# The filters' first transform step: one float32 product in place of three on hi + lo pairs

## The chip, the cores and the metric

The kernel runs on one core of a Trainium2 chip. The metric is the device time of one execution in microseconds. Five engines work side by side: TensorE (PE in the profile; its weight loads are PEld), VectorE (DVE), ScalarE (ACT), GpSimd (POOL) and SyncE (SP), which here issues most DMA transfers. Each engine takes its instructions in order.

## What is computed

One encoder block on 2048 tokens of width 1024: a combined input projection, attention on one half of the heads and a long convolution ("Hyena") on the other, an output projection, a mixture of experts and a gated embedding. The change lies in the long convolution's filters, which are made from weights alone and taken to the frequency domain:

```python
h = jnp.sin(freq2 * (h @ w_f2 + b_f2))
h = (h @ w_f3).reshape(L, HYENA_ORDER, 2, D_HYENA)       # L = 2048, order 2, 512 channels
h = h * decay[:, None, None, :]
h = h / (jnp.sum(jnp.abs(h), axis=0, keepdims=True) + EPS)
hf, hb = h[:, :, 0], h[:, :, 1]
circ = jnp.concatenate([hf[:1] + hb[:1], hf[1:], jnp.zeros_like(hf[:1]), hb[:0:-1]], axis=0)
return jnp.fft.rfft(circ, n=2 * L, axis=0)
```

## The kernel before, in words

A transform of 4096 points is done in two steps of matrix products: a first step over 128 points (the matrix `w1`, 128x128, the same for all columns) and a second step of small products with 32 matrices (`w2`). The filters' work is `stage_filter`: for each of eight groups (four blocks of 128 channels, two orders) `gen` makes eight tiles `g` of 128x512 float32 values (line 402) and sums their magnitudes (403), `norm` works out one over the sum and scales the eight tiles in place (lines 412 to 438; two tiles on VectorE, six on GpSimd, line 436, and last a correction of one row of tile 0, line 438), `fft1` is the first transform step and `fft2` the second. The parts of successive groups are interleaved: while `gen` makes group n, `fft1` works on group n - 1 and `fft2` on group n - 2.

TensorE multiplies in two modes here. A float32 operand is multiplied in full precision; such an instruction stands in the trace as two rows. A `float32r` operand is multiplied in one quick pass at less precision, and a product of nearly full precision is put together from three of them, on pairs hi + lo: hi*hi, lo*hi and hi*lo. `Kit.hi_lo` (lines 77 to 81) makes a pair: ScalarE casts the values to hi (line 80), and VectorE or GpSimd subtracts hi from the values (line 81). `fft1` does that for every tile `g` (pair `gh`, `gl`, one buffer each) and multiplies by the pair `w1h`, `w1l` of the matrix, which `hyena_consts` makes once; the three products gather in one PSUM bank (the tag `pm`, of which there is one for all the filter's work, `norm`'s small products among it), ScalarE copies the bank out (452) and a DMA writes it to DRAM (453).

At the same time runs the input projection, `stage_in`, in four quarters of 512 tokens: normalise and transpose the tokens (lines 168 to 178), then products on hi + lo pairs by three `float32r` matmuls at a time (lines 149 to 151), and for the convolution's channels a three-tap filter on VectorE (`acc`, lines 210 to 213) whose result TensorE transposes (220). The lo parts of its weights are made on GpSimd mostly (line 89). `interleave` writes the two sides' instructions in proportion to costs that they yield, and the framework's scheduler then sets the order on each engine. The Hyena stage (first product at line 505) needs the filters and the first channels; attention (741 onwards) comes from the projection's side.

Of the kernel before, what the change touches and what calls it, by code (L numbers as in the profile page):

```python
# [9 lines left out]
F32R = mybir.dt.float32r  # L10
# [8 lines left out]
P = 128  # L19
# [15 lines left out]
HB = 3  # L35
FI_LATE = 1.5
GB = 8
GHB = 1
RB, WB = 13, 8
LO_ENG = (0,)  # L40
LO_POOL = 0
# [278 lines left out]
def stage_filter(K, st, cns, consts, w_f1, b_f1, freq1, w_f2, b_f2, freq2, w_f3, bias, h_d, s_d):  # L320


    nc, tc = K.nc, K.tc
# [16 lines left out]
    with tc.tile_pool(name="fi_s", bufs=2, side=K.side) as ps_:  # L340
# [26 lines left out]
        for c in range(4):  # L367
            ps = psm.tile([P, 512], F32, tag="pm", name="ps")
# [6 lines left out]
            ps = psm.tile([P, 512], F32, tag="pm", name="ps")  # L375
# [8 lines left out]
    pw = pool("fi_w", 2)  # L384
# [56 lines left out]
    def fft1(o, b, st):  # L441
        for q in range(8):
            g = st["g"][q].rearrange("p a c -> p (a c)")
            gh = pw.tile([P, 512], F32R, tag="gh", name="gh", bufs=GHB)
            gl = pw.tile([P, 512], F32R, tag="gl", name="gl", bufs=GHB)
            K.hi_lo(gh, gl, g, nc.vector if q % 2 else nc.gpsimd)
            ps = psm.tile([P, 512], F32, tag="pm", name="ps")
            nc.tensor.matmul(ps, K.w1h, gh, start=True, stop=False)
            nc.tensor.matmul(ps, K.w1l, gh, start=False, stop=False)
            nc.tensor.matmul(ps, K.w1h, gl, start=False, stop=True)  # L450
            sg = pw.tile([P, 4, P], F32, tag="sg", name="sg")
            nc.scalar.copy(sg, ps.rearrange("p (a c) -> p a c", a=4))
            nc.sync.dma_start(s_d[o, b, :, q * 4:q * 4 + 4], sg)
            yield 0.9
# [19 lines left out]
    for n in range(10):  # L474
        b, o = n // 2, n % 2
        st = {}
        parts = [gen(o, b, st) if n < 8 else iter(()), one, two]
        for _ in range(8):
            for p in parts:
                yield next(p, 0.0)  # L480
        for p in parts:
            yield from p
        if n < 8:
            yield from norm(o, b, st)
        one, two = fft1(o, b, st) if n < 8 else iter(()), fft2((n - 1) % 2, (n - 1) // 2) if 0 < n < 9 else iter(())
# [102 lines left out]
def hyena_consts(K, pool, tmp, w1_c, w2_c, wb_c):  # L588
    nc = K.nc
    K.w1 = tmp.tile([P, P], F32, name="w1")  # L590
    K.w1h, K.w1l = [tmp.tile([P, P], F32R, name=f"w1{i}") for i in "hl"]
    K.w1d = pool.tile([P, P], F32, name="w1d")
    K.w2 = pool.tile([P, 32, 64], F32, name="w2")
    K.wb = pool.tile([P, 64], F32, name="wb")
    for t, c in ((K.w1, w1_c), (K.w1d[0:64], w1_c[0:64]), (K.w1d[64:128], w1_c[0:64]), (K.w2, w2_c), (K.wb, wb_c)):
        nc.sync.dma_start(t, c)
    K.hi_lo(K.w1h, K.w1l, K.w1)


class RopeTables:  # L600
# [23 lines left out]
class Attention:  # L624
# [15 lines left out]
    def pool(self, name, bufs, **k):  # L640
        return self.st.enter_context(self.K.tc.tile_pool(name=name, bufs=bufs, **k))
# [1153 lines left out]
def block_kernel(tc, A, out):  # L1795
# [11 lines left out]
    with ExitStack() as st:  # L1807
# [3 lines left out]
        s_hc, s_w = ExitStack(), ExitStack()  # L1811
        phc = s_hc.enter_context(tc.tile_pool(name="hc", bufs=1, side=K.side))
        consts = lambda tmp: hyena_consts(K, phc, tmp, A["c_w1"], A["c_w2"], A["c_wb"])
        W, ple = [], Ple(K, A["p"][0, 0], A["w_ple"][0], pp_d)
        K.filter_done = False
# [89 lines left out]
```

## Time and profile before

| | |
|---|---|
| median of 3 runs | 3180.53 us (3178.24 to 3187.92) |
| the profiled execution | 3189.39 us, its span 3187.4 us |
| TensorE busy over the span | 2893.6 us (91%) |
| VectorE, ScalarE, GpSimd busy | 2088.4, 1357.0, 1186.7 us |
| first and last product of the changed step | 142.3 and 636.0 us from the span's start |

The changed step lies between 140 and 640 us, a sixth of the span, and work of `stage_in` lies beside it all that time. A matmul's row in the trace shows how long it took from its start to its result; matmuls overlap, so what one costs TensorE is the time from its start to the start of the next.

### The profile page before, as it was taken

To read this page: it belongs to the slowest core of one execution; us is meant where nothing else is said; L and a number is where in the kernel's file an instruction comes from. 1 tells how busy PE (TensorE), PEld (TensorE's weight loads), DVE (VectorE), ACT (ScalarE), POOL (GpSimd) and SP (SyncE) were. 2 spreads that over 40 slices of the span, in tenths; PEclk is the share of its full clock that TensorE was granted. 3 is DMA by queue.
4 is the path that set the end of the run, shared out by engine and by line. 5 is a ranking of instruction groups with operands and counts; after the bars stand their busy time and mean duration, and the time that the engine had idled before them with its cause. 6 is when DMAs were issued, how large, how long until landed. Compare 5 with 4: busy or idle time off the path is not lost. (4 is left out here: it accounts for less than half of the span.)

```text
span 3187.4 us, 50724 instructions
## 1 busy us (share of the span) xinstructions
PE 2893.6 (91%) x19065; PEld 1942.2 (61%) x19065; DVE 2088.4 (66%) x2770; ACT 1357.0 (43%) x2040; POOL 1186.7 (37%) x1090
## 2 busy tenths in 40 slices
PE   7989898878899999759999999989999999998887
PEld 5767686655444453424444388866667777775766
DVE  5877767455687566527787644366667777775665
ACT  3343343432343334225444432245556666664332
POOL 1434544341365455228887543001111211221443
PEclk9999999888899999879999999989999999999998
DMA  6468797886656655651000254369789888997553
GB/s 195 145 205 254 229 276 216 229 267 199 200 176 180 190 163 167 179 170 32 18 18 10 65 167 142 140 216 320 249 275 351 293 300 285 308 333 245 178 179 112
DMA packets 471992, 627.48 MB, mean 197 GB/s; under 512 B 64597, under 2 KB 302984, under 8 KB 467262
## 3 DMA queue, kind: packets, MB, share of 16 engines
q1 hardware_dynamic: 451630, 568.73, 55.7%
q0 software_dynamic: 20112, 55.47, 5.4%
q8 instruction: 151, 2.47, 0.3%
q14 instruction: 99, 0.81, 0.1%
HBM read 462.45 MB, written 161.56 MB: 196 GB/s over the span
## 5 line engine op out<-in xcount | busy, mean ns | idle before, releaser
L1314 DVE TENSOR_TENSOR wl<-raw,wh 128x1024 fp32r<-128x1024 f32 x384 | 463.3, 1223 | 196.3 <-ACT wh L1309 187.5
L1309 ACT CAST wh<-raw 128x1024 fp32r<-128x1024 f32 x384 | 398.6, 1051 | 266.2 <-PE ps L1332 95.1
L829 POOL TENSOR_TENSOR sums<-e,sums 128x512 f32<-128x512 f32 x306 | 411.0, 1359 | 156.5 <-ACT e L810 152.1
L810 ACT ACTIVATE e<-ps 128x512 f32<-128x512 f32 x512 | 289.7, 597 | 345.7 <-PE ps L809 291.7
L743 DVE TENSOR_REDUCE mx<-pa 128x1 f32<-128x512 f32 x512 | 330.3, 682 | 111.7 <-PE pa L741 110.8
L819 PE MATMUL po<-e,v 128*64 128x512 f32 x1024 | 293.8, 627 | 3.5 <-ACT e L810 3.5
L1409 POOL DMA_DIRECT2D y_d<-ob x64 | 36.0, 565 | 590.0 <-DVE ob L1408 346.6
L1330 PE MATMUL ps<-wh,xt 128*128 128x512 f32 (+4 forms) x512 | 212.9, 416 | 6.8 <-ACT wh L1309 6.8
L1331 PE MATMUL ps<-wl,xt 128*128 128x512 f32 (+4 forms) x512 | 206.7, 404 | 5.9 <-DVE wl L1314 5.9
L1332 PE MATMUL ps<-wh,xt 128*128 128x512 f32 (+4 forms) x512 | 203.4, 397 | 0.0
L149 PE MATMUL ps<-xh,wh 128*128 128x512 f32 x384 | 155.4, 405 | 5.0 <-ACT U L205 5.0
L741 PE MATMUL pa<-kst,q 128*128 128x512 f32 x352 | 142.0, 454 | 18.3 <-DVE mx L743 12.9
L151 PE MATMUL ps<-xh,wl 128*128 128x512 f32 x384 | 154.4, 403 | 0.0
L150 PE MATMUL ps<-xl,wh 128*128 128x512 f32 x384 | 154.0, 401 | 0.0
L806 PE MATMUL ps<-q,kst 128*128 128x512 f32 x352 | 151.7, 431 | 0.0
L829 DVE TENSOR_TENSOR sums<-e,sums 128x512 f32<-128x512 f32 x110 | 123.9, 1133 | 35.4 <-ACT e L810 34.8
L809 PE MATMUL ps<-q,k 65*128 65x512 f32 x352 | 142.0, 403 | 4.8 <-DMA q<-mr 4.8
L89 POOL TENSOR_TENSOR wl<-raw,wh 128x2048 fp32r<-128x2048 f32 (+1 forms) x26 | 102.1, 3926 | 100.4 <-ACT wh L139 99.5
L741 PEld LDWEIGHTS pa<-kst,q 128*128 128x128 f32 x352 | 63.6, 193 | 121.9 <-DVE mx L743 66.8
L1336 PE MATMUL pr<-raw,xr 128*32 128x128 f32 (+1 forms) x2112 | 126.3, 303 | 1.6 <-DVE ob L1412 1.6
L1330 PEld LDWEIGHTS ps<-wh,xt 128*128 128x128 f32 (+4 forms) x512 | 95.6, 187 | 44.8 <-issue 14.3
L1279 POOL DMA_INDIRECT g<-h_d,idx x52 | 70.0, 1347 | 140.1 <-PE pt L1288 58.6
(379 smaller groups left out, 6761.0 us busy)
## 6 DMA issues: line engine op xcount, KB each, us to landing
raw<-in_w_gate_dram SPq DMA_DIRECT2D x128, 512.0 KB
raw<-in_w_up_dram SPq DMA_DIRECT2D x128, 512.0 KB
raw<-in_w_down_dram SPq DMA_DIRECT2D x128, 512.0 KB
h_f<-hs SPq DMA_DIRECT2D x256, 128.0 KB
ab<-h_f SPq DMA_DIRECT2D x32, 1024.0 KB
raw<-in_w_in_dram SPq DMA_DIRECT2D x30, 1024.0 KB
xt<-in_x_dram SPq DMA_DIRECT2D x32, 512.0 KB
dec<-in_c_decay_dram SPq DMA_DIRECT2D x64, 256.0 KB
```

Source lines behind the costliest of these rows:

```text
L149: nc.tensor.matmul(ps, lh, rh, start=(k == 0), stop=False)
L151: nc.tensor.matmul(ps, ll, rh, start=False, stop=(k == 7))
L741: nc.tensor.matmul(pa, qh[:, t * P:(t + 1) * P], self.kst[g][:, q * 512:(q + 1) * 512], start=True, stop=True)
L743: nc.vector.tensor_reduce(out=mx[:, t, q:q + 1], in_=pa, axis=AX.X, op=ALU.max)
L810: nc.scalar.activation(out=pe[:, i], in_=ps, func=AF.Exp, scale=0.125)
L819: mm = nc.tensor.matmul(po[H2[i]], v[:, kt, g * 64:(g + 1) * 64], pe[:, i], start=(kt == 0), stop=(kt == NT - 1), skip_group_check=True)
L829: acc[j][1].tensor_tensor(out=sums[j], in0=pe[:, i], in1=src, op=ALU.add)
L1309: nc.scalar.copy(hi, raw)
L1314: nc.vector.tensor_tensor(out=lo, in0=raw, in1=hi.bitcast(F32), op=ALU.subtract)
L1330: nc.tensor.matmul(ps[:m], xt[:, k, 0, :m], hv[:, j], start=(k == 0), stop=False)
L1331: nc.tensor.matmul(ps[:m], xt[:, k, 0, :m], lv[:, j], start=False, stop=False)
L1332: nc.tensor.matmul(ps[:m], xt[:, k, 1, :m], hv[:, j], start=False, stop=(k == 7))
```

## The change

The tile `g` goes to TensorE as it is, with `w1` as it is, in one float32 product. The pairs, their buffers and the two pairs of `w1` are gone, and with them 64 casts on ScalarE, 32 subtractions each on VectorE and GpSimd, and 192 matmuls, for which 64 float32 ones (128 rows of a trace) stand.

```diff
     def fft1(o, b, st):
         for q in range(8):
             g = st["g"][q].rearrange("p a c -> p (a c)")
-            gh = pw.tile([P, 512], F32R, tag="gh", name="gh", bufs=GHB)
-            gl = pw.tile([P, 512], F32R, tag="gl", name="gl", bufs=GHB)
-            K.hi_lo(gh, gl, g, nc.vector if q % 2 else nc.gpsimd)
             ps = psm.tile([P, 512], F32, tag="pm", name="ps")
-            nc.tensor.matmul(ps, K.w1h, gh, start=True, stop=False)
-            nc.tensor.matmul(ps, K.w1l, gh, start=False, stop=False)
-            nc.tensor.matmul(ps, K.w1h, gl, start=False, stop=True)
+            nc.tensor.matmul(ps, K.w1, g, start=True, stop=True)
             sg = pw.tile([P, 4, P], F32, tag="sg", name="sg")
...
 def hyena_consts(K, pool, tmp, w1_c, w2_c, wb_c):
     nc = K.nc
     K.w1 = tmp.tile([P, P], F32, name="w1")
-    K.w1h, K.w1l = [tmp.tile([P, P], F32R, name=f"w1{i}") for i in "hl"]
...
-    K.hi_lo(K.w1h, K.w1l, K.w1)
```

The scheduler sets a new order on every engine of the first stage. Lines of the changed kernel are one less than those of before up to line 443, and the product is its line 444.

TensorE at the second group, from the last product that `norm`'s sums need to the first products of `fft1`. Before:

```order
L420 MATMUL ps<-hb,rowb 128x128
...
L176 MATMUL pt<-ident,xn 128x128 x8
L422 MATMUL ps_1167<-acc,blk 1x128
L423 MATMUL ps_1167<-hb,rowb 1x128
...
L448 MATMUL ps<-gh,w1h 128x512
L449 MATMUL ps<-gh,w1l 128x512
L450 MATMUL ps<-gl,w1h 128x512
L176 MATMUL pt<-ident,xn 128x128 x8
L448 MATMUL ps<-gh,w1h 128x512
```

And now:

```order
L419 MATMUL ps<-hb,rowb 128x128
L175 MATMUL pt<-ident,xn 128x128 x4
...
L421 MATMUL ps_1115<-acc,blk 1x128
L422 MATMUL ps_1115<-hb,rowb 1x128
...
L444 MATMUL ps<-g,w_549 128x512 x3
L175 MATMUL pt<-ident,xn 128x128 x8
L294 MATMUL pd<-zt,w_551 64x128 x16
L444 MATMUL ps<-g,w_549 128x512
```

The first "..." of before holds 10 matmuls of the projection (128x256), the second 24; now the first holds 12 and the second 12. So fewer products stand between `norm`'s sums and the first product that needs a scaled tile, and three products of `fft1` follow one another with nothing between. Two groups of the eight have such a row of three. At all eight groups, counted from line 423 (now 422) to the first product of `fft1`, the projection's matmuls between are 34, 24, 27, 47, 24, 26, 47 and 24 before and 31, 12, 22, 20, 1, 49, 17 and 0 now; transposes and products of `gen` and `fft2` stand there too.

VectorE a little ahead of that place (`part` and `acc` are `gen`'s sums and the projection's three-tap filter). Before:

```order
L403 TENSOR_REDUCE part<-g 128x128
L226 COPY stg<-pt 128x4x128
L81 TENSOR_TENSOR gl<-g,gh 128x512
L402 TENSOR_TENSOR g<-pd,dec 128x512
L403 TENSOR_REDUCE part<-g 128x128
L210 TENSOR_SCALAR acc<-U,cw 128x512
```

And now:

```order
L402 TENSOR_REDUCE part<-g 128x128
L225 COPY stg<-pt 128x4x128
L401 TENSOR_TENSOR g<-pd,dec 128x512
L402 TENSOR_REDUCE part<-g 128x128
L209 TENSOR_SCALAR acc<-U,cw 128x512
```

The subtraction is gone from the middle; what stood behind it, the three-tap filter among it, is as it was.

## Rows read from the trace of the kernel before

**Rows 1.** Stretches: us, busy us of each engine (instructions), granted clock, DMA share, GB/s.

```profile
100.00:200.00 100.00, 85.17 (x624) 65.45 (x622) 86.77 (x97) 33.85 (x52) 42.23 (x49) 0.97 0.49 156
200.00:300.00 100.00, 92.47 (x863) 77.53 (x864) 70.15 (x76) 40.83 (x64) 45.20 (x41) 0.97 0.84 251
300.00:400.00 100.00, 82.83 (x686) 64.52 (x686) 78.53 (x85) 38.18 (x60) 47.84 (x53) 0.93 0.76 230
400.00:500.00 100.00, 96.45 (x898) 80.16 (x898) 66.78 (x72) 44.22 (x67) 42.08 (x39) 0.97 0.91 270
500.00:640.00 140.00, 115.16 (x980) 94.68 (x977) 86.40 (x90) 53.80 (x89) 58.91 (x56) 0.93 0.77 223
```

**Rows 2.** What TensorE waited for, 100 to 700 us: total us, times, longest.

```profile
PE pt L220 <- DVE acc L213: 26.8, 17, 5.7
PE ps L448 <- ACT gh L80: 9.0, 4, 3.5
PE ps L450 <- POOL gl L81: 7.7, 5, 2.5
PE ps L151 <- DVE xl L81: 6.8, 4, 2.0
PE ps L450 <- DVE gl L81: 4.8, 3, 3.1
```

**Rows 3.** Instruction groups of the changed step: busy us, mean ns, idle before.

```profile
L448 PE MATMUL ps<-gh,w1h 128*128 128x512 f32 x64 | 30.6, 478 | 10.6 <-ACT gh L80 9.0 <-ACT sg L452 1.5
L80 ACT CAST gh<-g 128x512 fp32r<-128x512 f32 x64 | 39.7, 621 | 99.4 <-DVE g L438 37.9 <-PE ps L449 37.0 <-POOL gl L81 14.6
L81 POOL TENSOR_TENSOR gl<-g,gh 128x512 fp32r<-128x512 f32 x32 | 48.9, 1529 | 62.0 <-ACT gh L80 55.3 <-PE ps L151 6.4 <-PE ps L450 0.3
L81 DVE TENSOR_TENSOR gl<-g,gh 128x512 fp32r<-128x512 f32 x32 | 30.1, 941 | 33.8 <-ACT gh L80 22.9 <-PE ps L450 10.8
L452 ACT COPY sg<-ps 128x512 f32<-128x512 f32 x64 | 37.6, 588 | 39.0 <-DMA s_f<-sg 17.9 <-PE ps L450 15.3 <-issue 5.0
```

**Rows 4.** TensorE in order of time at 188 us: start us, us, instruction [idle before].

```profile
188.14 0.28 PE L151 MATMUL ps<-wh,xl 128*128 128x256 f32 x1
188.26 0.40 PE L448 MATMUL ps<-gh,w1h 128*128 128x512 f32 x1
188.50 0.39 PE L449 MATMUL ps<-gh,w1l 128*128 128x512 f32 x1
188.73 0.40 PE L450 MATMUL ps<-gl,w1h 128*128 128x512 f32 x1
```

**Rows 5.** TensorE in order of time at 1238 us: one float32 product (L841).

```profile
1237.94 0.39 PE L809 MATMUL ps<-q,k 65*128 65x512 f32 x1
1238.26 1.04 PE L841 MATMUL pa<-osq,sel 128*32 128x512 f32 x2
1239.23 0.73 PE L741 MATMUL pa<-kst,qh 128*128 128x512 f32 x2
1239.89 1.13 PE L505 MATMUL ph<-z,w1d 64*128 64x512 f32 x4
```

**Rows 6.** TensorE in order of time at 203 us, head of the second group.

```profile
202.99 0.28 PE L151 MATMUL ps<-wh,xl 128*128 128x256 f32 x1
206.79 0.79 PE L448 MATMUL ps<-gh,w1h 128*128 128x512 f32 x1 [3.52 <-ACT gh L80]
```

**Rows 7.** VectorE at the same place, first and last of `norm`'s scaling.

```profile
196.37 0.95 DVE L426 RECIPROCAL inv<-inv 128x128 f32<-128x128 f32 x1
...
204.80 1.23 DVE L438 TENSOR_TENSOR g<-g,iv 1x128 f32<-1x128 f32 x1
```

**Rows 8.** VectorE, GpSimd and TensorE in order of time, 174 to 182 us.

```profile
174.56 4.36 DVE L210 TENSOR_SCALAR acc<-U,cw 128x512 f32<-128x512 f32 x1 [0.21 <-ACT U L205]
...
174.12 4.51 POOL L89 TENSOR_TENSOR wl<-raw,wh 128x2048 fp32r<-128x2048 f32 x1 [4.65 <-ACT wh L139]
...
181.57 1.12 PE L220 MATMUL pt<-ident,acc 128*128 128x128 f32 x4 [5.25 <-DVE acc L213]
```

**Rows 9.** All instructions of line 210: duration ns min/median/max, first and last start us.

```profile
L210 DVE TENSOR_SCALAR acc<-U,cw x48: 531/546/4445, 85.5 to 794.6; 128x513 f32<-128x513 f32 x36, 128x512 f32<-128x512 f32 x12
```

**Rows 10.** TensorE in order of time, first product of the Hyena stage.

```profile
695.90 1.09 PE L505 MATMUL ph<-z,w1d 64*128 64x512 f32 x2 [0.66 <-DMA raw<-in_w_in_dram]
```

More of the change, by code (lines that the diff above doesn't have):

```diff
@@ L37 @@
 GB = 8
-GHB = 1
 RB, WB = 13, 8
```

## The prediction

> **What bounds the kernel now.** I began with the stretches of 100 us, to see which engine is full where the changed step runs. From 100 to 640 us [rows 1] TensorE is busy 472 of 540 us; VectorE comes next with 389, ScalarE and GpSimd are less than half full. The five stretches are not alike: from 200 to 300 and 400 to 500 us TensorE is busy 92 and 96 of 100 us, and each us of matmul added there should be a us of time; in the other three it is idle for a sixth of the time and VectorE is nearly as busy. The whole first stage hangs on TensorE's queue, since what follows (line 505, attention) needs its products. So I count by what the change adds to that queue and what it takes out of its waits. Idle time of the other engines is worth nothing until TensorE waits for it.
>
> Next I read what TensorE waits for [rows 2]. The largest wait is for the three-tap filter on VectorE, 26.8 us. The changed step has three: 9.0 us for the cast `gh`, 7.7 and 4.8 for the subtraction `gl`. Last I read the groups of the step itself [rows 3]: ScalarE's casts are 39.7 us, the subtractions 48.9 on GpSimd and 30.1 on VectorE, 119 us of work that goes. But most of what these engines do here is idle time anyway; the casts' queue alone stood 99.4 us before them.
>
> **TensorE's work: +17 us.** Three `float32r` products of 512 columns, one behind the other, start at 188.26, 188.50 and 188.73 [rows 4]: 0.235 us each, 0.70 us for the three, 64 times 45 us. What takes their place is a float32 product of 512 columns. None with all 128 rows into all 128 columns of the array is in the trace; the nearest uses 128 rows into 32 columns, the next 64 rows into 128. The first starts at 1238.26 and the next instruction at 1239.23 [rows 5]: 0.97 us. It started 0.09 us later than the row ahead (1237.94) and its 0.235 us would have it, and the two `float32r` products behind it take 0.66 us to the next float32 one where 0.47 would do, so a change between the two kinds costs some 0.1 us. Alone among `float32r` products the new one thus costs 0.97 + 0.2 = 1.17 us. It does not always stand alone: `gen`, `fft2` and the transposes are float32 too, and counted over the new order up to line 505 the kinds change 217 times, where they changed 231 times. So 64 x 0.97 = 62 us, less 14 x 0.1, is 61 us: 16 us more than the 45. The granted clock of 0.93 to 0.97 [rows 1] stretches that to 17. The upper end is 64 x (1.17 - 0.70) = 30, if most stand alone; the lower 16.
>
> The Trainium skill ("FP8 and Floating Point Precision", TensorE Precision Notes) says that a true float32 product goes through the array in four passes, against this change. By that rule and the pass of rows 4 the product would cost 4 x 0.235 = 0.94 us and the term would be 64 x 0.24, some 15 us; the row has 0.97 and the term stays.
>
> **Waits for the subtraction: -12 us.** The third product waited 7.7 + 4.8 us for `gl` [rows 2], and nothing takes its place. The bounds are -12.5 and about -6: where VectorE was late because its whole queue was late, the wait moves to the next thing that TensorE needs from it.
>
> **Waits at the head of a group: +4 us.** The 9.0 us for `gh` are not the cast's. At the second group TensorE stood 3.52 us from 203 on [rows 6], and VectorE's scaling of the tiles, begun at 196.37, ended only at 206.03 with line 438 [rows 7]; the cast behind it (0.62 us [rows 3]) is all that the change takes out, 2.5 us over the four waits. Line 444 waits for line 438 as the cast did. And the new order puts less in front of it: at the second, fifth and eighth group, where it waited before, 12, 23 and 24 fewer matmuls of the projection, at 0.12 us (half of 0.235; 188.14 to 188.26 [rows 4]) 1.4 to 2.9 us each, some 7 us. That is +4 or 5 together. Bounds: -2.5 (VectorE's chain is no longer behind) and +10 (groups three, four and seven, which also lose cover, begin to wait). I take +4. While line 444 waits, the projection's products behind it on TensorE wait too, and the transposes of the next tokens with them.
>
> **Waits for the one bank: +3 us.** Two groups now have three products of `fft1` in a row. All of them write the one bank `pm`, so the second and third must wait until ScalarE has copied the one before out: 0.59 us [rows 3] and 0.16 us until the result is there (0.40 less 0.235 [rows 4]), with the hand-overs some 0.85 us, four times. Bounds 0 and +5.
>
> **VectorE's relief: -4 us.** VectorE loses 30.1 us of work and 33.8 us of standing before it [rows 3], 64 of 540 us, an eighth. If its lateness falls by as much, TensorE's waits for lines 213 and 81, 33.6 us [rows 2], fall by 4. Bounds 0 and -13. I don't take more, because the largest of these waits have another cause: line 210 takes 0.55 us as a rule and up to 4.45 [rows 9], and the 5.25 us wait at 176 us comes from one that took 4.36 us while GpSimd worked at a weight subtraction of 4.51 us [rows 8]. Those subtractions (line 89) stay.
>
> The Trainium skill ("SBUF — State Buffer", SBUF: two separate sides) says that GpSimd and some forms of VectorE instruction take a shared pair of ports in turn, each for a whole instruction. The trace agrees in rows 8. By that rule the 32 subtractions that leave GpSimd would free VectorE too, but only where one of them stood in its way.
>
> **The rest: -2 us or nothing.** Where TensorE waits for something that no product of its own has to come before, added work fits into the wait: it is idle for 68 of 540 us [rows 1], an eighth of 17. ScalarE's and GpSimd's relief is hidden behind TensorE at no gain; their releases in rows 2 are counted above. Transfers are the same in number and size. The matrix's own pair is two small instructions at the start, and its load is long done at 142 us. Behind 700 us TensorE's order is nearly the same row for row, so what is won or lost at the start is carried to the end.
>
> **The sum:** 17 - 12 + 4 + 3 - 4 - 2 = +6 us. The profiled execution took 3189.39 us, 9 above the median of its runs; the difference of one execution carries over to the median: 3180.5 + 6 = 3186.5 us, say 3186. A measurement of this kernel can tell about 0.3% from no change, some 9.5 us, so my forecast is no change, on the slower side.
>
> **Rivals.**
> - *TensorE is the bound nearly throughout, and the new product is dearer than its nearest row.* For it: 92 and 96% busy in two stretches [rows 1], and the upper price of 30 us. With -12, +6 at the heads, +3 at the bank and nothing from VectorE it is +27 us, 3207; with the product at 1.0 us in place of 0.97, which is 2 us more, heads at +10 and nothing from VectorE, it is 19 - 12 + 10 + 3 - 2 = +18, 3198. It decides from about 3 us above my sum. Against it: most new products stand beside other float32 work.
> - *VectorE and the waits for the pairs were the bound.* It ends on the other side. For it: three of five stretches have VectorE at 62 to 87% [rows 1], and it stood 22.9 us waiting for `gh` and 10.8 for a free `gl` [rows 3], in a queue where the three-tap filter stands behind. If the waits for lines 213 and 81 fall by 13 us, the heads by 2.5 and the bank costs nothing: 16 - 12.5 - 2.5 - 13 - 2 = -14, 3166; with a little of the clock that the shorter waits give back (0.93 to 0.97 granted [rows 1], some 24 us lost in 540; a fifth of it) -19, 3162. It decides if VectorE's relief passes 15 us. Against it: the slow rows of line 210 stay, and the new order takes cover away.
> - *The change does what it says and no part meets the end:* the first stage's gain or loss is taken up where the Hyena stage waits for its transfers later. That is no change as well, 3180, and I count it with the forecast.
>
> **How the numbers follow.** No change 0.40 (the forecast and the third rival, 3171 to 3190); the first rival, slower, 0.38, centred on 3199; the second, faster, 0.22, centred on 3164. The likeliest case's own range is 3171 to 3190. With one in ten left out on each side the range is 3163 to 3208: the lower end is the second rival, the upper the first at its dearest.
>
> **What would show it.** In the changed profile line 444 should have 128 rows and 0.97 to 1.17 us from one product to the next instruction; a start-to-start of 1.3 us would make it slower. The waits on `gl` should be gone, a wait of line 444 for VectorE of 8 to 14 us stand in place of that for the cast, and one of some 3 us for the copy of line 452. The wait of line 220 for VectorE should still be above 15 us; if it falls below 10, the second rival holds. The first row of line 505, at 695.9 us before [rows 10], should come within 10 us of that; if it doesn't move but the time does, the cause lies behind and my account is wrong.

## The result: faster by half a per cent, and not where the change was made

| | before | after |
|---|---|---|
| median | 3183.21 us (10 runs) | 3170.03 us (10 runs, 3161 to 3179 without one) |
| ratio after / before | | 0.9947, 95% interval 0.9935 to 0.9959 |
| profiled execution, span | 3189.39, 3187.4 us | 3178.87, 3177.1 us |

One of the ten runs (3276 us, at a clock of 0.847 where the others had 0.95 to 0.96) is left out of the ratio. The forecast was no change, 3186 us; the kernel is 0.53% faster, outside the 0.3%, though inside the range.

**What the profile after shows of the changed step.** First the stretches of the kernel after (us, busy us of PE, PEld, DVE, ACT and POOL with instructions, granted clock, DMA share, GB/s), which answer to [rows 1]:

```profile
100.00:200.00 100.00, 86.24 (x578) 62.36 (x576) 83.03 (x96) 25.72 (x36) 43.17 (x48) 0.91 0.53 164
200.00:300.00 100.00, 91.69 (x878) 72.89 (x881) 51.22 (x60) 34.72 (x55) 19.97 (x16) 0.90 0.84 255
300.00:400.00 100.00, 85.19 (x600) 61.98 (x590) 74.25 (x75) 27.95 (x36) 44.14 (x56) 0.90 0.69 207
400.00:500.00 100.00, 92.39 (x878) 73.05 (x879) 53.44 (x65) 37.64 (x61) 23.65 (x20) 0.93 0.87 270
500.00:640.00 140.00, 119.48 (x908) 88.72 (x907) 84.25 (x91) 45.84 (x66) 45.44 (x62) 0.90 0.76 226
```

TensorE is busy 475 of 540 us, as before (472). VectorE has 346 in place of 389, ScalarE 172 in place of 211. The granted clock, 0.93 to 0.97 before, is 0.90 to 0.93 now. Next TensorE's waits from 100 to 700 us (total us, times, longest), for [rows 2]:

```profile
PE ps L444 <- DVE g L437: 19.6, 7, 6.1
PE ps L444 <- ACT sg L446: 13.5, 7, 3.8
PE pt L219 <- DVE acc L212: 9.4, 7, 2.9
PE ps L418 <- DVE acc L411: 8.3, 4, 3.4
```

The 12.5 us on `gl` are gone, and the wait for the three-tap filter fell from 26.8 to 9.4. In their place stand the head of a group (19.6 us, where the cast had 9.0), the one bank (13.5, where it had 1.5) and `norm`'s products, which wait for VectorE's sums (8.3, where they had 1.6). All told TensorE is idle for 65 of the 540 us; before it was 68. Third, TensorE in order of time:

```profile
165.38 1.02 PE L444 MATMUL ps<-g,w 128*128 128x512 f32 x2
165.84 0.79 PE L150 MATMUL ps<-xh,wl 128*128 128x512 f32 x1
166.47 0.39 PE L148 MATMUL ps<-xh,wh 128*128 128x512 f32 x1
...
170.82 1.02 PE L444 MATMUL ps<-g,w 128*128 128x512 f32 x2
171.77 1.10 PE L394 MATMUL pd<-w,h 64*64 64x128 f32 x32
...
195.77 2.06 PE L444 MATMUL ps<-g,w 128*128 128x512 f32 x2 [4.27 <-DVE g L437]
198.64 2.05 PE L444 MATMUL ps<-g,w 128*128 128x512 f32 x2 [0.81 <-ACT sg L446]
201.45 2.05 PE L444 MATMUL ps<-g,w 128*128 128x512 f32 x2 [0.77 <-ACT sg L446]
...
700.30 2.42 PE L499 MATMUL ph<-z,w1d 64*128 64x512 f32 x4 [1.60 <-DMA z<-uc_d]
```

Where a float32 instruction follows, the product takes 0.95 us to the start of the next (170.82 to 171.77), the price of [rows 5]. Among `float32r` products the next one starts 0.46 us after it, but then takes 0.79 us in place of 0.39; the one after that starts 1.09 us after the product, and less the 0.235 us of the one between, the product costs 0.85. So the time to the next start, by which this document prices a matmul, is too low there, and has to be read one instruction further on. At the second group the wait for VectorE comes as foretold, the clock falls behind it (the same product now lasts 2.05 us), and two waits of 0.8 us for the bank follow.

The Hyena stage starts at 700.30, 4.4 us *later* than in [rows 10]. That is not quite like for like: 44 products of the projection, 16 of line 699 and 8 transposes, which stood ahead of that mark before, stand behind it now. The first place behind the changed step up to which both kernels have done the same instructions on TensorE (the step's own products left out) is at some 760 us. A row soon behind it is easily found, a product of the projection that waits for ScalarE. Before and after:

```profile
777.55 0.79 PE L149 MATMUL ps<-xh,wh 128*128 128x512 f32 x1 [5.02 <-ACT U L205]
...
787.29 0.80 PE L148 MATMUL ps<-xh,wh 128*128 128x512 f32 x1 [4.06 <-ACT U L204]
```

Here the changed kernel is 9.7 us late, and 2.2 us in a second trace of it; the mean is what the sum said, +6. All that makes this execution 10 us shorter came after it.

**Where the time came from.** To see that, the table below gives how much later (+) or earlier (-) TensorE starts its work than in the trace of before: the start of an instruction in the one trace less that of the same instruction (the n-th of its line) in the other, as the median over all that lie within 12 us of the time at the head of the column. One trace each; two traces of one kernel differ by 9 us at 860 us and by up to 17 at the end. The column 778 is the start of the one product just shown. All kernels of the study are in it. The column "late order" says whose order TensorE has behind some 800 us (below). From there to the end, 667 of its 13,584 instructions stand in another place in the changed kernel (outside the longest common order), nearly all of them before 1300 us and from 2050 to 2250 us; in the kernel with pairs in (1,0) and in that with float32 in blocks 2 and 3 it is none.

| kernel | late order | ratio, 95% interval | 778 | 860 | 1300 | 1750 | 1830 | 2240 | end |
|---|---|---|---|---|---|---|---|---|---|
| after | after | 0.9947 (0.9935 to 0.9959) | +9.7 | +3.6 | +1.9 | +2.3 | -5.0 | -11.3 | -10.2 |
| after, second trace | after | 0.9951 (0.9932 to 0.9970) | +2.2 | -5.1 | -12.5 | -12.1 | -19.5 | -22.8 | -26.9 |
| float32 in seven groups, pairs in (2,0) | after | 0.9949 (0.9932 to 0.9966) | +6.1 | -4.3 | -8.6 | -10.3 | -16.2 | -22.3 | -19.1 |
| float32 in seven groups, pairs in (1,0) | before | 1.0013 (0.9997 to 1.0029) | +0.2 | 0.0 | +4.4 | +6.7 | +5.2 | +0.6 | +5.3 |
| half: float32 in blocks 0, 1 | after | 0.9903 (0.9887 to 0.9920) | -3.9 | -13.2 | -16.7 | -17.3 | -21.5 | -29.1 | -23.2 |
| the same, second trace | after | 0.9883 (0.9864 to 0.9901) | -5.3 | -11.7 | -3.1 | -2.0 | -6.1 | -14.6 | -11.5 |
| half: float32 in blocks 2, 3 | before | 0.9999 (0.9984 to 1.0014) | -2.5 | -6.1 | -2.4 | -1.0 | -2.6 | -5.4 | -2.3 |
| half: float32 in order 1 | after | 0.9944 (0.9927 to 0.9962) | +1.7 | -8.3 | -7.6 | -5.0 | -13.6 | -17.8 | -13.2 |
| pairs, two buffers each | after's behind 900, but for two rows | 0.9929 (0.9908 to 0.9950) | -9.0 | -11.7 | -10.8 | -10.2 | -8.5 | -12.5 | -12.6 |
| the same, casts moved | after's behind 900, but for two rows | 0.9948 (0.9928 to 0.9967) | -4.5 | -6.5 | -8.8 | -7.5 | -10.1 | -13.2 | -14.3 |
| half (blocks 0, 1), two buffers | after's behind 900 | 0.9882 (0.9861 to 0.9904) | -9.1 | -13.8 | -13.0 | -13.9 | -21.2 | -27.2 | -21.9 |
| before, casts moved | before | 0.9998 (0.9985 to 1.0011) | +0.4 | -1.8 | +4.0 | +4.7 | +3.4 | +4.1 | -0.3 |
| before, two rows swapped | before | 1.0004 (0.9992 to 1.0017) | +2.1 | -0.1 | +0.7 | +2.9 | +0.8 | -0.2 | -1.3 |
| before, transposes moved | before, but for the mixture of experts | 0.9997 (0.9983 to 1.0011) | +2.6 | 0.0 | +4.2 | +2.8 | +0.1 | +0.5 | +6.7 |
| before, all three moved | before, but for the mixture of experts | 0.9976 (0.9962 to 0.9991) | +0.4 | -1.9 | -1.8 | -3.4 | -6.0 | -10.5 | -9.1 |
| after, product issued twice | a fourth | 1.0052 (1.0030 to 1.0074) | +29.1 | +20.0 | +17.7 | +17.8 | +15.1 | +10.8 | +15.9 |
| after, pairs made but not used | a fifth | 0.9992 (0.9980 to 1.0004) | - | -1.6 | -12.8 | -2.1 | -2.8 | -3.4 | +1.7 |

In the first row 7.3 us are won between 1750 and 1830 us, the end of attention, and 6.3 up to 2240 us, the start of the mixture of experts. At the first of these places the trace of before has this (ScalarE, then TensorE, in order of time):

```profile
1797.68 1.08 ACT L810 ACTIVATE e<-ps 128x512 f32<-128x512 f32 x2 [0.53 <-issue]
1805.93 0.62 ACT L80 CAST th<-ya 128x512 fp32r<-128x512 f32 x1 [7.17 <-DMA ya<-ya_d]
1806.77 0.62 ACT L80 CAST th<-ya 128x512 fp32r<-128x512 f32 x1 [0.21 <-DMA ya<-ya_d]
1807.29 3.03 ACT L810 ACTIVATE e<-ps 128x512 f32<-128x512 f32 x6
...
1807.93 2.46 PE L819 MATMUL po<-e,v 128*64 128x512 f32 x4 [3.50 <-ACT e L810]
```

Two casts of the output projection stand in ScalarE's queue ahead of 14 of attention's exponentials and wait 7.17 us for a transfer; the exponentials behind them wait too, and TensorE for those. In the changed kernel the scheduler has put the same casts ahead of the last 6 only, and TensorE does not wait there in either of its traces. No line of the diff is near these; the scheduler, which sets the order of the whole program, had come to another one.

**The theories.** *Late order*: the gain is that of the order in which the scheduler set the instructions behind the first stage; the changed step is worth nothing by itself. *First stage*, the rival: the cheaper step and VectorE's relief are worth the 13 us, wherever a trace shows them. *Luck*, the second rival: transfers that landed earlier by chance.

### The profile page after: what moved, and what is told of

Its sections match the earlier page's. It is cut to its first block, busy times and chain, and to the rows that moved or that the text cites. A ratio compares the mean times of both kernels' runs of the same rounds, so it can differ in the third digit from the quotient of the medians.

```text
span 3177.1 us, 50424 instructions
## 1 busy us (share of the span) xinstructions
PE 2905.4 (91%) x19001; PEld 1937.3 (61%) x19001; DVE 2047.3 (64%) x2737; ACT 1322.0 (42%) x1975; POOL 1143.2 (36%) x1058
## 5 line engine op out<-in xcount | busy, mean ns | idle before, releaser
L148 PE MATMUL ps<-wh,xh 128*128 128x256 f32 x384 | 121.6, 317 | 4.7 <-ACT xh L79 2.4
```

The source lines that it names most:

```text
L148: nc.tensor.matmul(ps, lh, rh, start=(k == 0), stop=False)
```

## The experiments

**The changed kernel again, and one group more or less.** When the float32 product is used in some groups only, TensorE's order behind about 800 us (the last 3500 matmuls of attention and the start of the mixture of experts) comes out either as in before or as in after, row for row, and which one does not go by how many groups are changed. (That holds for TensorE. In the kernels with the late order of before, ScalarE and VectorE have some 150 rows each in another place behind 1300 us.)

> The changed kernel once more, for a second trace. Late order (the 10 us were won behind the changed step, because the scheduler set another order at the end of attention and at the start of the mixture of experts): the time is 3161 to 3173 again, the trace is again 2 to 5 us behind the kernel before at 700 us and at 1200 us, and gains 5 to 8 us at about 1800 us and 5 to 8 us between 2090 and 2210 us. First stage (the cheaper pairs and the relief of VectorE were worth it): the time is the same, but the gain is there by 1200 us. Luck (transfers that by chance landed earlier in one profiled execution): the steps at 1800 and 2200 us are not there again, or at other places.

> Seven of the eight groups have the float32 product, one (block 1, order 0) keeps its pairs. The orders behind the first stage (end of attention, start of the mixture of experts, everything after) are the ones of before, row for row. Late order: nothing is won late, and the first stage costs what it cost in the changed kernel, some +2 to +4 us: 3181 to 3189, a ratio of 0.999 to 1.002. First stage: seven eighths of the gain, 3168 to 3175, a ratio of 0.995 to 0.997. Luck: anything between.

> Seven groups with the float32 product and one with pairs, as in the earlier run of seven groups, but the one that keeps its pairs is block 2, order 0, in place of block 1, order 0. By that the order of the last 3500 matmuls of attention and the start of the mixture of experts is the one of the changed kernel and not of before. Late order: the gain is there, ratio 0.993 to 0.997, where the other gave 1.0013. First stage: the two are alike, both near 1.001.

```diff
-            nc.tensor.matmul(ps, K.w1, g, start=True, stop=True)
+            if (b, o) == (1, 0):
+                gh = pw.tile([P, 512], F32R, tag="gh", name="gh", bufs=GHB)
...
+                nc.tensor.matmul(ps, K.w1h, gl, start=False, stop=True)
+            else:
+                nc.tensor.matmul(ps, K.w1, g, start=True, stop=True)
```

That is the kernel with pairs in (1, 0), with the code of before between; the other has (2, 0) there.

Seven eighths of the change with the late order of before: 1.0013. Seven eighths with the late order of after: 0.9949, the whole gain. TensorE's waits in order of time, first of the kernel with pairs in (1,0):

```profile
1192.21 3.69 PE L308 MATMUL ph<-ab,wa 64*64 64x128 f32 x64 [6.13 <-issue]
...
1789.32 0.63 PE L844 MATMUL pa<-sums,sel 128*32 128x512 f32 x3 [2.31 <-POOL sums L832]
1815.65 1.56 PE L822 MATMUL po<-e,v 128*64 128x512 f32 x4 [2.44 <-ACT e L813]
...
2117.12 1.09 PE L1291 MATMUL pt<-ident,g 128*128 128x128 f32 x4 [7.17 <-DMA g<-h_d,idx]
```

and of the kernel with pairs in (2,0), the same stretches:

```profile
1806.04 1.65 PE L844 MATMUL pa<-sums,sel 128*32 128x512 f32 x6 [0.73 <-DVE sums L832]
...
2099.65 1.94 PE L1291 MATMUL pt<-ident,g 128*128 128x128 f32 x8 [4.37 <-DMA g<-h_d,idx]
```

The first has the waits of before at their places (there 4.5, 1.8, 3.5 and 4.9 us), the second those of after, where of the four only the gather's is left (3.6 and 5.3 us). The first stage theory falls here: at 778 us the kernel that wins is 5.9 us behind the other. Luck falls too: the stall near 1186 us stands in every trace with the late order of before and unchanged rows (4.5 to 6.5 us) and in none with that of after. One thing did not come as expected: the second trace of after was not 2 to 5 us behind, but 12.5 ahead at 1300 us. It had won 14.7 us since 778, where the first trace had won 7.8.

**Half and half, three ways.**

> Half and half, first of a pair: the float32 product for the four groups of blocks 2 and 3, pairs for those of blocks 0 and 1. On TensorE the order of the last 3500 matmuls of attention and of all behind it is the one of the kernel before. Late order (the gain comes from the orders behind 860 us, not from the first stage): no gain, ratio 0.999 to 1.002. First stage: half of the gain, ratio 0.997 to 0.998.

> Half and half, second of the pair: the float32 product for the four groups of blocks 0 and 1, pairs for those of blocks 2 and 3, so as many of each as in the first. The order of the last 3500 matmuls of attention and at the start of the mixture of experts is the one of the changed kernel. Late order: nearly the whole gain, ratio 0.994 to 0.997, and the steps in drift against before lie at 860 to 1240, near 1800 and between 2090 and 2210 us. First stage: half of the gain like the other half, ratio 0.997 to 0.998, and no difference between the two.

> Half and half in a third way: float32 for the four groups of order 1, pairs for those of order 0; the order late in the program is that of the changed kernel. Late order: a gain as of the half with blocks 0 and 1 (0.9903): 0.989 to 0.996. First stage: half the gain, 0.997 to 0.998. If half and half is better in the first stage than all float32, the drift at 860 us is again -8 to -13 us, where the changed kernel has +4 and -5.

The edit is the one above with `b < 2`, `b >= 2` or `o == 0` for the pairs. The pair of equal halves gave 0.9999 and 0.9903, the third 0.9944: again by the late order. From the row at 778 us to the end, the six traces with the late order of after gain 19 us on average (19.9, 29.1, 25.2, 19.3, 6.2 and 14.9); the three with that of before and rows unmoved lose 2 (0, 5.1 and 0.2). That is 21 us; by the ratios, whose means are 0.9930 and 1.0004, it is 24. By place, the difference is 7 us from 778 to 860 us, 4 from 860 to 1300, 5 from 1750 to 1830 and 3.5 from 1830 to 2240. I had not expected that half and half would be clearly better than the changed kernel.

**No changed product at all.**

> The kernel before with pairs in all groups and one number changed: two buffers for each of the pair tiles. The end of attention stands as in before (the casts of the out-projection ahead of 14 exponentials), the middle of attention and the mixture of experts in another order, the latter that of the changed kernel. Late order: most of the gain without the changed product, less the 3 to 7 us near 1800 us: ratio 0.995 to 0.998. First stage: a second buffer can only take away part of the 9.0 us wait for the cast: 0.998 to 1.000.

> The kernel before with pairs in all groups, the casts at the end of attention put where the changed kernel has them, and two buffers for each of the pair tiles (in place of one), by which the scheduler sets the order of the mixture of experts and of all behind it to that of the changed kernel. Late order: both late steps are won, 10 to 15 us, and the first stage is at most 5 us better or worse than before by the second buffer: 3166 to 3175, ratio 0.995 to 0.998. First stage: the late places are worth nothing, and the buffer at most removes part of the 9.0 us wait for the cast: 3178 to 3184, ratio 0.998 to 1.000. Luck: like the first stage.

```diff
-GHB = 1
+GHB = 2
...
-        K.hi_lo(th[:, 0:4], tl[:, 0:4], ya, nc.gpsimd)
+        c = nc.scalar.copy(th[:, 0:4], ya)
+        if t < 2:
+            K.behind(c, K.es[-7])
+        nc.gpsimd.tensor_tensor(out=tl[:, 0:4], in0=ya, in1=th[:, 0:4].bitcast(F32), op=ALU.subtract)
```

The first of them has the first line alone, the second both. With pairs in all groups and one buffer more they give 0.9929 and 0.9948, as much as the change, without it; the first is better than the 0.995 to 0.998 expected of both. At 778 us they are 9.0 and 4.5 us ahead, and behind it they win 3.6 and 9.8, so a good part of their gain is the second buffer's, in the first stage. TensorE's order behind 900 us is that of after but for two rows at the end of attention, and there, from 1750 to 1830 us, they won at most 2.6 us, where the kernels with all of that order won 4.1 to 8.6.

**The named waits one by one.** Which rows of the late order are it? Three edits of the kernel before, each meant to move only what I held to be the cause, and all three together. The swap does so. With the casts the scheduler also moved 163 of ScalarE's rows behind 1750 us, and with the transposes 149 of TensorE's rows in the mixture of experts.

> The kernel before, with pairs in all groups, and one edit at the end of attention: the first two casts of the out-projection's tokens on ScalarE are put behind the seventh exponential from the end, where the changed kernel has them (6 exponentials behind the first cast and not 14). Late order: TensorE's wait for an exponential at 1808 us (3.5 us, and a lower clock behind it) is gone and the time falls by 5 to 8 us, to 3174 to 3178, ratio 0.9975 to 0.9985; the step in drift at 1800 us is there with no change at 140 to 640 us. First stage: no change, 3183, ratio 1.000 within 0.001. Luck: no change either.

> The kernel before with one pair of neighbouring rows on VectorE in the other order: at about 1187 us the scaling of attention's fifth output (ob<-ob,gcol, which waits for a transfer) is put behind the Hyena product ab<-ab,ph that stood behind it. TensorE's order is the one of before. Late order, by the mechanism of a queue in which one instruction waits for a transfer and holds up the next: TensorE's wait of line 308 at 1186 us (4.5, 6.1, 6.5 and 5.1 us in the four traces with that order) falls below 2 us, and the drift against before steps by -3 to -6 us between 1180 and 1300 us; ratio 0.998 to 0.9995. If the wait only moves to the next transfer: no step, ratio 1.000.

> The kernel before with one edit at the start of the mixture of experts: the first transposes of the second gathered tokens on TensorE, which wait for the gather (4.9 to 9.0 us in the five traces with the order of before, 3.6 to 5.3 with that of the changed kernel), are put behind the first 16 of the products pr<-raw,xr, as in the changed kernel. By the named waits: the stall at 2105 us is 3 us shorter, and the drift against before steps by -3 to -5 us between 2050 and 2240 us; ratio 0.9985 to 0.9995. By the order as a whole: no step of more than 1.5 us, ratio 1.000.

> The kernel before with the three named corrections at once: the swap of two rows on VectorE at 1187 us, the two casts at the end of attention behind 8 more exponentials, and the transposes at the start of the mixture of experts behind 16 products. Pairs in all groups, the first stage as before. By the named waits: the sum of what the changed kernel won at these places, some -4, -5 and -4 us: ratio 0.995 to 0.997. By the order as a whole (each wait that is taken away here comes back a few rows on): at most -4 us, 0.9985 to 1.000.

```diff
+            if K.no == 5:
+                K.behind(gate, K.abs[47])
...
+                if K.nt == 9:
+                    K.behind(tr, K.prs[15])
```

The casts' edit is the one shown above. Here `gate` is attention's fifth `ob<-ob,gcol` and `K.abs[47]` the product `ab<-ab,ph` that stood behind it; `tr` is the first transpose of the second gathered tokens, `K.prs[15]` the 16th product `pr<-raw,xr`.

The swap at 1187 us shows best how such an edit can fail. VectorE and TensorE of before, in order of time:

```profile
1187.52 0.75 DVE L858 SCALAR_TENSOR_TENSOR ob<-ob,gcol 128x512 f32<-128x512 f32 x1 [6.65 <-DMA ob<-r_d]
1188.19 2.35 DVE L529 TENSOR_TENSOR ab<-ab,ph 128x1024 f32<-128x1024 f32 x2
...
1190.64 3.69 PE L308 MATMUL ph<-ab,wa 64*64 64x128 f32 x64 [4.49 <-issue]
```

and with the two rows swapped:

```profile
1182.94 2.35 DVE L531 TENSOR_TENSOR ab<-ab,ph 128x1024 f32<-128x1024 f32 x2 [0.37 <-PE ph L297]
1189.58 0.75 DVE L860 SCALAR_TENSOR_TENSOR ob<-ob,gcol 128x512 f32<-128x512 f32 x1 [4.29 <-DMA ob<-r_d]
1190.25 1.28 DVE L745 TENSOR_REDUCE mx<-pa 128x1 f32<-128x512 f32 x2
...
1187.78 1.98 PE L310 MATMUL ph<-ab,wa 64*64 64x128 f32 x64
1190.99 1.10 PE L743 MATMUL pa<-kst,q 128*128 128x512 f32 x2 [1.24 <-DVE mx L745]
```

Line 308 no longer waits, but the transfer is as late as it was, and what now stands behind the waiting instruction is the row maximum `mx`, for which TensorE waits next. From 1180 to 1300 us the step was 1.0 us, where 3 to 6 were expected; the time, 1.0004, shows none. The casts, of which 5 to 8 us had been expected, gave 0.9998: the wait at 1808 us is gone, and 20 us ahead of it TensorE stands 4.44 us where it stood 1.83 before:

```profile
1787.93 1.07 PE L842 MATMUL pa<-sums,sel 128*32 128x512 f32 x3 [4.44 <-POOL sums L830]
```

The transposes alone gave 0.9997. All three at once gave 0.9976 (7.7 us of 3193), between the two ranges expected and half of the changed kernel's gain, without a row of the first stage moved; of the wait for the gather (4.9 to 9.0 us with the late order of before, 3.6 to 5.6 with that of after) 1.59 are left (TensorE of that kernel):

```profile
1779.72 0.63 PE L846 MATMUL pa<-sums,sel 128*32 128x512 f32 x3 [2.88 <-POOL sums L834]
...
2107.78 1.07 PE L1299 MATMUL pt<-ident,g 128*128 128x128 f32 x8 [1.59 <-DMA g<-h_d,idx]
...
2113.40 0.51 PE L1344 MATMUL ps<-wh,xt 128*128 128x512 f32 x1 [3.11 <-ACT wh L1323]
```

So the named waits, with the rows that the scheduler moved along with them, are some 8 of the 21 us. About 4 more lie with a wait of TensorE at 1018 us (shown in the last section): between 999 and 1028 us each of the six traces with the late order of after wins 4.2 us. The rest lies with rows that I have not named.

**The first stage by itself.** Two kernels with the changed product: one issues each product twice (twice the step's work, the same output), one makes the pairs as before and uses them for nothing.

> The changed kernel with every product of the first step issued twice, the second over the first (the output is the same, the work of the step doubled): 64 more products at 0.97 us by the prediction, 62 us of TensorE. It asks how much of the first stage's work reaches the end. If it reaches it in full: the first product of the Hyena stage some 55 to 65 us later, and the time 3215 to 3235, ratio 1.008 to 1.015. If the stretches from 640 to 860 us take up a part, as they took up 8 us in the run with seven groups: 8 to 10 us less than at that first product. The order behind 860 us is partly that of the changed kernel, so up to 15 us may come off.

> The changed product, but the pairs are still made (casts and subtractions) and used by nothing: it leaves out the relief of the other engines and keeps the dearer product. The order behind 860 us is a third one, neither that of before nor of the changed kernel. If VectorE's relief is what paid for the dearer product in the first stage (TensorE's wait for the three-tap filter fell from 26.8 to 9.4 us in the changed kernel): that wait is again above 20 us, and the drift at 860 us is +8 to +20 us. If the relief is not the cause: the wait stays near 10 us and the drift at 860 us within 5 us of the changed kernel's (+4 and -5). The time itself tells little, since the late order is another.

The stretch from 100 to 640 us of after, of its second trace and of the kernel with the product twice:

```profile
100.00:640.00 540.00, 474.99 (x3826) 358.99 (x3825) 346.18 (x383) 171.88 (x254) 176.37 (x201) 0.91 0.74 224
...
100.00:640.00 540.00, 469.34 (x3895) 355.43 (x3894) 347.62 (x383) 175.58 (x258) 176.26 (x202) 0.93 0.75 228
...
100.00:640.00 540.00, 493.17 (x3820) 352.97 (x3820) 348.67 (x373) 166.77 (x243) 175.56 (x199) 0.97 0.71 217
```

Some 60 us of TensorE's work moved the Hyena stage's first product to 721.0 us, 24 later than the mean of the two traces of after (700.3 and 693.8), where 55 to 65 had been one end of the expectation. The rows show where the rest went: TensorE is busy 18 to 24 us more, so it is idle for less, and the granted clock is 0.97 where it was 0.91 and 0.93. At a mean of 0.97 the lower of its two levels (1.2 GHz of 2.4) held 7% of the time, at 0.91 and 0.93 it held 18 and 14%: 61 and 37 us less, worth 31 and 19. Together that is an estimate of 43 to 49 of the 60 us. Against the mean of the two traces of after, the 24 us are 23 at 778 us, 21 at 860 and 23 at 1300.

With the pairs made for nothing the wait for the three-tap filter came back (TensorE's waits, 100 to 700 us):

```profile
PE pt L220 <- DVE acc L213: 22.4, 12, 4.0
PE ps L448 <- ACT sg L450: 9.3, 9, 2.2
PE ps L448 <- DVE g L438: 8.8, 5, 3.6
```

That speaks for VectorE's relief as what had taken it away in the changed kernel. It does not go by the number of subtractions, though: of the halves, with as many each, float32 in blocks 0 and 1 has 8.8 us of this wait and float32 in order 1 has 22.9. And the drift at 860 us was -1.6, not the +8 to +20 expected: the waits for the bank and the head, the other two rows, were smaller than in the changed kernel by about as much.

**The best version.**

> Half and half (float32 for blocks 0 and 1, pairs for blocks 2 and 3) with two buffers for each pair tile. Two buffers alone gave 0.9929 and were 11.7 us ahead at 860 us, half and half alone 0.9903 and 13.2 us ahead. If the two gains of the first stage are of different waits they add: 15 to 20 us ahead at 860 us, ratio 0.985 to 0.990. If both come from where attention's preparation and the Hyena stage happen to be at 700 to 860 us: 8 to 14 us ahead, ratio 0.990 to 0.995.

> Half and half with blocks 0 and 1 in float32 once more, for a second trace: was its lead of 13.2 us at 860 us that of the kernel or of one execution? Of the kernel: -9 to -16 us again, ratio 0.989 to 0.992. Of the execution: near the changed kernel's +4 and -5 us, and a ratio of 0.993 to 0.996, like the changed kernel.

Half and half was ahead by 11.7 us at 860 us in its second trace too: that lead belongs to the kernel. With two buffers it was 13.8, so the two leads do not add, though the ratio fell into the range expected if they did. At 0.9883 and 0.9882 these two beat both kernels, with medians of 3162 and 3157 us beside 3193 for the kernel before on the same chip; the runs do not tell them apart.

## Why the prediction was wrong

**The step that failed** is the last one ahead of the sum: "Behind 700 us TensorE's order is nearly the same row for row, so what is won or lost at the start is carried to the end." Nearly the same was not enough, and TensorE's order was not the only one to read: from 800 us on 667 of its 13,584 instructions stand elsewhere, and so do 245 of ScalarE's 1585 and 259 of VectorE's 2129. Among the rows that cost or won time are a cast ahead of eight exponentials on ScalarE, and on VectorE a scaling ahead of a product and a sum beside GpSimd's. With the late order of before kept, seven eighths and half of the change give 1.0013 and 0.9999, which is the forecast; with the late order of after, the change in whole or in part gives 0.9883 to 0.9951. The test written down for it decided: the first product of the Hyena stage moved by +4.4 and -2.1 us in the two traces of after, and the row at 778 us by +9.7 and +2.2, the time by -13, so the cause lies behind. From 778 us on the new order is worth some 20 us, against the 2 to 10 that the step costs.

**The terms**, from the first trace of after:

- *The product*, 0.97 us each and 1.17 alone among `float32r` products: measured 0.95 next to float32 instructions, but 0.85 alone, so the extra price for a change between the two kinds is not there. The term of +17 also took nearly all the work for time. The doubled product shows 24 us for 60 of TensorE's work here; at that rate, an estimate, 16 us of it cost some 6.
- *The subtraction*, -12: the waits are gone, 12.5 us.
- *The heads*, +4 with an upper bound of +10: 19.6 for 9.0 us, so +10.6, just beyond the bound (23.1 in the second trace). *The bank*, +3 with an upper bound of +5: 13.5 us in seven waits for 1.5 of the old step, +12. Four waits in two groups had been counted from the rows where three products follow each other; the bank also holds up products that stand alone.
- *VectorE's relief*, -4 with a bound of -13: the waits for lines 213 and 81 fell from 33.6 to 9.6 us, -24. The slow rows of line 210 had been taken for its main cause, and they are still there (up to 4.66 us, where it was 4.45); with the pairs made for nothing the wait for line 213 is 22.4 us again, so the subtractions in VectorE's queue have a part in it. How much is theirs and how much the new order's is not shown.
- *The clock* had no term of its own: 0.95 on average before, 0.91 and 0.93 in the two traces of after, with longer waits at the heads and the bank.

The bank and the relief are off by 9 and 20 us in opposite senses, and yet the sum of +6 stands beside +9.7 and +2.2 at 778 us. That is partly luck. It may be that the waits of this stage take each other's place, so that their sum is steadier than its terms: TensorE is idle for 65 to 71 of the 540 us in before, in both traces of after and with the pairs made for nothing.

**The rivals.** The faster one had the sign, and half of its mechanism: VectorE's relief did pass the 15 us from which it was to decide, and decided nothing, since heads and bank took it back. The slower one had the heads right, but the product was cheaper than its nearest row, not dearer. The third, that the Hyena stage takes up what the first stage wins or loses, is not borne out: of the doubled product's 24 us, 23 were there at 778 us and at 1300. The kernels with two buffers began the Hyena stage 15.5 and 19.4 us earlier (680.4 and 676.5 us) and were only 4.5 and 9.0 ahead at 778, but some 36 instructions that had stood ahead of its start stood behind it in them.

What stays open: the rows that make the rest of the late gain, and why half and half, with the same late order, is 8 to 12 us ahead of the changed kernel at 860 us.

## What to carry to other kernels

Where a scheduler sets the order, a local change is two changes: the edit, and a new order of everything behind it, which here was worth some 20 us where the edit cost 2 to 10. Compare the order of *every* engine to the end of the program before a term is called carried through, time a stage by a place up to which both kernels have done the same work, and look above all at instructions that wait for a transfer in an in-order queue: what is queued behind them decides what they cost. To measure an edit by itself, vary it in ways that keep the later order (one group more or less was enough), and take a gain that comes with another order for what it is, to be had in other ways too.

## What the runs showed of the hardware

The kernel with the most work for TensorE from 100 to 640 us had the highest granted clock there: 0.97 with 493 us busy of 540, against 0.91 and 0.93 with 475 and 469 in the two traces of after, and some 60 us of products cost 24. Whether the work raised the clock or the new order did is not shown: the kernel before has 0.95 with 472 us busy, and the wait at the heads is 9.7 us with the product twice, where it was 19.6.

A float32 product of 128 rows into 128 columns, 512 columns wide, cost 0.85 us between `float32r` products and 0.95 next to float32 instructions, at the full clock. Its two rows last 1.02 us together at the full clock and 2.05 at half of it.

A VectorE sum, 0.67 us at its shortest, took 6.85 beside GpSimd. VectorE, GpSimd and TensorE of before, in order of time:

```profile
1009.82 1.28 DVE L736 TENSOR_TENSOR ql<-pa,qh 64x512 fp32r<-64x512 f32 x2 [1.26 <-ACT qh L735]
1011.03 6.85 DVE L829 TENSOR_TENSOR sums<-e,sums 128x512 f32<-128x512 f32 x1
...
1011.14 2.52 POOL L693 TENSOR_TENSOR dup<-raw,sq 128x512 f32<-128x512 f32 x2
1013.61 3.71 POOL L829 TENSOR_TENSOR sums<-e,sums 128x512 f32<-128x512 f32 x3
...
1018.53 0.73 PE L741 MATMUL pa<-kst,qh 128*128 128x512 f32 x1 [4.09 <-DVE mx L743]
```

It ended 0.56 us behind the last of *five* GpSimd instructions that ran without a gap (1011.14 to 1017.32). The Trainium skill ("SBUF — State Buffer", SBUF: two separate sides) has, of a GpSimd instruction that reads SBUF and a VectorE one with two operands there, whichever starts first hold the shared ports for the whole instruction and the other blocked; these rows agree that VectorE was blocked, and add that it got no turn between one GpSimd instruction and the next. Who started first can't be read from them: VectorE's row begins 0.11 us ahead of the first of the five, but still overlaps the row before it on VectorE. TensorE's wait behind it is 4.08 or 4.09 us in all seven traces with the late order of before and in none with that of after.
